# Input products of a triangular inverse as 64x64 matmuls in place of 64x32 quarters

## The chip, the cores and the metric

The kernel runs on one core of one Trainium2 chip. The metric is the device time of one launch in microseconds (us): the median of three runs is 1617.11 us (1615.75 to 1618.56). TensorE (PE) multiplies matrices into PSUM, VectorE (DVE), ScalarE (ACT) and GpSimd (POOL) do the elementwise work, SyncE (SP) issues DMAs. Each engine takes its instructions strictly in the order in which they stand in its queue, and waits on semaphores for the others.

## The reference, cut to what matters

Two transformer-like blocks follow each other on 512 tokens of width 1024. The first has a mixer with a convolution branch and a recurrence (RWKV, 8 heads of width 64, both directions, over 256 context tokens and then 512 tokens); the second has another recurrence, windowed attention and a feed-forward part. The change touches the recurrence of the first:

```python
def wkv_scan(state0, r, decay, kk, b, v, k, reverse):
    def step(S, inp):
        r_t, w_t, kk_t, b_t, v_t, k_t = inp
        sa = jnp.einsum("bhvk,bhk->bhv", S, kk_t)
        S = (S * w_t[:, :, None, :] - sa[..., None] * b_t[:, :, None, :]
             + v_t[..., None] * k_t[:, :, None, :])
        return S, jnp.einsum("bhvk,bhk->bhv", S, r_t)
```

The kernel does 64 tokens at a time (a chunk; 12 chunks, the first 4 of context). Inside a chunk the steps depend on each other through a 64x64 strictly triangular matrix A = (keys kk) x (b), and the chunk needs the inverse of (1 + A). The result is the same function; only how A is computed and stored changes.

## The kernel before, in words

Heads are taken two at a time: `j` = 0 to 3, one head in partitions 0 to 63, the other in 64 to 127. For each `j` there are two pieces of work.

`prep(j)` makes the inputs: decays and keys for both directions `d` (activations on ACT, a scan and some products on DVE, into `KB` and `KR`), then the products for the inverse (line 633, PSUM tile `pa`), and then calls `inverse(j)`. A is stored in quarters of 32x32: the two blocks on the diagonal go to `AKD`, the two off it to `AKO`, for 24 matrices (12 chunks, 2 directions). Every quarter is a matmul of its own: 64 rows of contraction, 32 output rows, 32 columns. Twelve chunks by two quarters by two heads are 48 matmuls, then ACT copies the PSUM tile out (line 638), once for `AKD` and once for `AKO`. `AKO` has two buffers, `AKD` one.

`inverse(j)` inverts the diagonal 32x32 blocks by 31 steps of substitution on DVE (lines 670 and 671, two instructions a step, 124 of each for the four `j`), between a transpose into `U` (line 662) and two out of `X` (`F1`, `F2`, lines 673 and 674), and then forms the off-diagonal block with two rounds of 32x32 matmuls (`pt`, lines 691, from `AKO` and `F2`, copied by ACT to `T`; and `po`, lines 698 and 699), copied into `XT`.

`stage(j)` runs the recurrence with the finished inputs: 12 groups, each one chunk of both directions, as a chain matmul, ACT copy `RU` (line 756), matmul with `XT`, ACT copy `RU` (762), matmul, ACT copy into the state `S` (768). All its matmuls go through `mmh` (line 644): two 64x64 matmuls, one a head. For every second group `pair` makes scores (`psc`, masked by a DVE copy into `AS`, line 731) and transposes (`pkt`, copied by ACT to `kbt`).

`prep(0)` and the start of `prep(1)` run beside the projections of `proj`, which are 128x128 matmuls. The rest of `prep(1)`, and `prep(2)`, run beside stage 0, `prep(3)` beside stage 1. Both generators are cut by `yield`s into steps; `stage` takes `RB` = 4, 2, 1, 1 steps after each group of stages 0 to 3, with priorities, and a scheduler then orders each engine's queue. When the inverse of `prep(3)` is done, its memory becomes the pools of the next phase: `ada12` streams 32 weight tiles of 512 KB (line 539) and reduces each with one DVE instruction (line 540) beside stages 2 and 3, and the loads of the output projection `wout` (line 156) stand behind them in SP's queue.

Of the kernel before, what the change touches and what calls it, by code (L numbers as in the profile page):

```python
# [10 lines left out]
F32 = mybir.dt.float32  # L11
# [7 lines left out]
P = 128  # L19
# [103 lines left out]
class K:  # L123
# [120 lines left out]
    def build(self):  # L244
        tc = self.tc
        with ExitStack() as es:
            self.dr = es.enter_context(tc.tile_pool(name="dr", bufs=1, space=bass.MemoryType.DRAM))
            self.ea = es.enter_context(ExitStack())
            p0 = self.p0 = self.pool(es, "p0", side="left")
            self.cst = p0.tile([P, NCST], F32, name="cst")  # L250
            self.vec = p0.tile([P, NVEC], F32, name="vec")
            self.mod = p0.tile([P, 48, 2], F32, name="mod")
            self.scz = p0.tile([P, KD, 32], F32, name="scz")
            self.mhalf = p0.tile([P, 16], F32, name="mhalf")
            zxb = p0.tile([P, KD, NX], F32, name="zx")
            self.zx = [zxb[:, k, :] for k in range(KD)]
            with ExitStack() as er:
                r0 = self.r0 = self.pool(er, "r0", side="left")
                self.sg = r0.tile([P, NX], F32, name="sg")
                self.vD = self.dr.tile([P, 4, 12, 64], F32, name="vD")  # L260
                self.rD, self.kD, self.kkD = [[self.dr.tile([P, n], F32, name=f"{t}D{j}") for j in range(4)] for t, n in (("r", NX), ("k", NT), ("kk", NT))]
                st = lambda p, name, shape: p.tile([P] + shape, F32, name=name)
                XT0, XT1 = self.XT0, _ = st(r0, "XT0", [24, 64]), zxb[:, 5:8, :].rearrange("p a (b c) -> p (a b) c", c=64)
                set0 = {"KB": [st(r0, f"KB0{d}", [12, 2, 64]) for d in range(2)], "KR": [st(r0, f"KR0{d}", [1280]) for d in range(2)]}
                self.sets = [dict(set0, XT=XT0), {"XT": XT1}, None, dict(set0, XT=XT0)]
                self.hb, self.kah = st(r0, "hb", [16]), st(r0, "kah", [4, 4])
                with ExitStack() as ep:
                    self.pp = self.pool(ep, "pp", side="right")
                    self.lin = [self.pp.tile([P, NT], F32R, name=f"lin{i}") for i in range(2)]

                    room = [(f"KB1{d}", 6) for d in range(2)] + [("KR10", 5)]
                    self.room = []
                    for tag, n in room:
                        t = self.pp.tile([P, n, NC_], F32, tag=tag, name="adaw", bufs=1).rearrange("p a b -> p (a b)")
                        self.room += [t[:, i * 512:i * 512 + 512].unsqueeze(1) for i in range(n // 2)]
                    self.psp = self.psum(ep, "psp", side="right")
                    self.AKD = st(self.pp, "AKD", [32, 32])
                    with ExitStack() as e1:
                        self.wp = self.r1 = self.pool(e1, "r1", side="left")
                        self.ps = self.psum(e1, "ps1")  # L280
                        self.mmbufs, self.axbufs, self.wbufs, self.wsbufs = 4, 2, 4, 3
                        self.proj()
                    r2 = self.r2 = self.pool(er, "r2", side="left")
                    self.ps2 = self.psum(er, "ps2")
                    self.sets[2] = {"KB": [st(r2, f"KB2{d}", [12, 2, 64]) for d in range(2)], "KR": [st(r2, f"KR2{d}", [1280]) for d in range(2)], "XT": st(r2, "XT2", [24, 64])}
                    self.rwkv(es, ep)
            self.tail()
# [11 lines left out]
    def proj(self):  # L299
        nc, A, r1, p0 = self.nc, self.A, self.r1, self.p0  # L300
# [47 lines left out]
        for kc in range(KD):  # L348
# [4 lines left out]
            for i in range(2):  # L353
# [5 lines left out]
                    nc.gpsimd.tensor_tensor(out=hlo[i][kc], in0=xT[i][kc], in1=hhi[i][kc].bitcast(F32), op=ALU.subtract)  # L359
                else:  # L360
                    nc.vector.scalar_tensor_tensor(out=hlo[i][kc], in0=xT[i][kc], scalar=sh, in1=hhi[i][kc].bitcast(F32), op0=ALU.add, op1=ALU.subtract)
        nc.gpsimd.memset(self.AKD, 0.0)

        def tile_of(u, x=True, c=True):
            ws = [ahead.pop((u, k0), None) or piece(u, k0) for k0 in (0, 4)]
# [15 lines left out]
        for i, t in enumerate(self.lin):  # L381
            r = slice(64 * i, 64 * i + 64)
# [60 lines left out]
        for tb in range(6):  # L443
            t = r1.tile([P, NX], F32, tag="vs", name="v", bufs=4)
            nc.scalar.activation(out=t, in_=pv[tb], func=AF.Copy)
            for i in range(4):
                r, hs = slice(64 * (i % 2), 64 * (i % 2) + 64), slice(64 * (i // 2), 64 * (i // 2) + 64)
# [6 lines left out]
        for j in range(4):  # L454
            t = self.zx[j]
# [89 lines left out]
    def prep(self, j):  # L545
        nc, pp = self.nc, self.pp
# [22 lines left out]
        nc.scalar.activation(out=bo, in_=pb, func=AF.Copy)  # L569
        S["bo"] = bo  # L570
        ch = lambda t: t.rearrange("p (c t) -> p c t", t=64)
        AKO = S["AKO"] = pp.tile([P, 24, 32], F32, tag="AKO", name="AKO", bufs=2)
        for d in range(2):
            def lora(i, out, bias):

# [46 lines left out]
            nc.vector.tensor_tensor(out=krx[:, :, 1, :], in0=ch(rt), in1=inc[:, 4:12, :], op=ALU.mult)  # L622
            yield

            for off, A in enumerate((self.AKD, AKO)):
                pa = psm(384, "pa")
                for c in range(12):
                    kp = krc[:, c, :] if c < 4 else krx[:, c - 4, 0, :]
                    lt, rt_ = (kp, kb[:, c, bs, :]) if d else (kb[:, c, bs, :], kp)
                    for q in range(2):  # L630
                        o, i = 32 * q, 32 * (q ^ off)
                        for h in (0, 64):
                            nc.tensor.matmul(pa[h + o:h + o + 32, c * 32:c * 32 + 32], lt[h:h + 64, o:o + 32], rt_[h:h + 64, i:i + 32], start=True, stop=True)
                    if c == 5:
                        yield
                self.copy(nc.scalar, A[:, 12 * d:12 * d + 12, :], pa.rearrange("p (c t) -> p c t", t=32))
                yield
        yield from self.inverse(j)

# [14 lines left out]
    def inverse(self, j):  # L654

        nc, pp = self.nc, self.pp
        big = lambda name: pp.tile([P, 32, 32], F32, tag="inv", name=name, bufs=3)
        XT, AKO = self.S[j]["XT"], self.S[j]["AKO"]  # L660
        U, tmp, X = big("U"), big("tmp").rearrange("p a b -> p (a b)"), big("X")
        nc.vector.transpose(out=U, in_=self.AKD.rearrange("p n i -> p i n"))
        nc.gpsimd.memset(X, 0.0)
        nc.gpsimd.memset(X.rearrange("p a b -> p (a b)")[:, ::33], 1.0)
        for k in range(31):
            if k % 4 == 0:
                yield
            n, w = 31 - k, k + 1
            tv = tmp[:, 0:n * w].rearrange("p (a b) -> p a b", b=w)
            nc.vector.tensor_tensor(out=tv, in0=U[:, k + 1:32, k:k + 1].to_broadcast([P, n, w]), in1=X[:, k:k + 1, 0:w].to_broadcast([P, n, w]), op=ALU.mult)  # L670
            nc.vector.tensor_tensor(out=X[:, k + 1:32, 0:w], in0=X[:, k + 1:32, 0:w], in1=tv, op=ALU.subtract)
        F1, F2 = big("F1"), big("F2")
        nc.vector.transpose(out=F1.rearrange("p n i -> p i n"), in_=X)
        nc.vector.transpose(out=F2.rearrange("p n j -> p j n"), in_=X.rearrange("p i j -> p j i"))
        yield
        b0, b1 = [slice(o, o + 32) for o in (0, 64)], [slice(o + 32, o + 64) for o in (0, 64)]
        D = slice(0, 12), slice(12, 24)
        for r, F in zip(D, (F1, F2)):
            self.copy(nc.vector, XT[:, r, :].rearrange("p n (q i) -> p n q i", q=2), F[:, r, :].unsqueeze(2).to_broadcast([P, 12, 2, 32]))
        for h in range(2):  # L680
            nc.gpsimd.memset(XT[b1[h], D[0], 0:32], 0.0)
            nc.gpsimd.memset(XT[b0[h], D[1], 32:64], 0.0)

        T = big("T")
        ps = lambda name: self.psp.tile([P, 12, 32], F32, tag="inv", name=name, bufs=1)
        for r in D:
            yield
            pt = ps("pt")
            for n in range(r.start, r.stop):
                for h in range(2):  # L690
                    nc.tensor.matmul(pt[b1[h], n - r.start, :], AKO[b0[h], n, :], F2[b0[h], n, :], start=True, stop=True)
            for h in range(2):
                self.copy(nc.scalar, T[b1[h], r, :], pt[b1[h]])
        yield
        po = ps("po")
        for c in range(12):
            for h in range(2):
                nc.tensor.matmul(po[b0[h], c, :], T[b1[h], c, :], F1[b1[h], c, :], start=True, stop=True)
                nc.tensor.matmul(po[b1[h], c, :], F1[b1[h], 12 + c, :], T[b1[h], 12 + c, :], start=True, stop=True)
        for h in range(2):  # L700
            self.copy(nc.scalar, XT[b0[h], D[0], 32:64], po[b0[h]], -1.0)
            self.copy(nc.scalar, XT[b1[h], D[1], 0:32], po[b1[h]], -1.0)
# [692 lines left out]
```

## Time and profile before

| what | value |
|---|---|
| median of three runs | 1617.11 us |
| profiled execution: its time, its span | 1620.11 us, 1618.3 us |
| mean granted PE clock over the span | 0.969 |
| busy: PE, DVE, ACT, POOL | 1533.4, 998.3, 629.8, 116.8 us |
| `proj` with `prep(0)`, until the first group of stage 0 | 0 to 261 us |
| stage 0, stage 1, stage 2, stage 3 | 261 to 338, 338 to 430, 430 to 492, 492 to 551 us |

The span runs from the first instruction to the last; 1.8 us of the execution's time lie outside it. A granted clock of 1.00 is TensorE's level of 2.4 GHz, 0.50 is 1.2 GHz. A PE that the profile calls busy has a matmul in flight; that doesn't say that the array is full. A row of the timeline merges neighbours of one form: start, duration, engine, line, operation, out<-in, array rows*columns of a matmul, shape, count, and in brackets the idle time before it with what ended it.

### The profile page before, as it was taken

The numbers are of one execution on the slowest core, as the hardware profiler recorded it, in microseconds if no ns is written. First come the engines' busy times: TensorE is split into PE (matmuls) and PEld (weight loads), VectorE is DVE, ScalarE is ACT, GpSimd is POOL, SyncE is SP. The second block draws the span as 40 slices with busy tenths as digits, with TensorE's granted clock in tenths as the row PEclk, the third lists the DMA queues.
The fourth block names the chain that finished last, engine by engine and source line by source line (L and its number), as shares of the span: only waits on it lengthen the run. The fifth ranks groups of instructions, "written<-read, shape, count | busy, mean of one in ns | idle before, by whom it ended". The sixth has DMA issues, their size and how long they took to land. (4 is left out here: it accounts for less than half of the span.)

```text
span 1618.3 us, 31205 instructions
## 1 busy us (share of the span) xinstructions
PE 1533.4 (95%) x13214; PEld 1254.0 (77%) x13214; DVE 998.3 (62%) x1689; ACT 629.8 (39%) x1258; POOL 116.8 (7%) x133
## 2 busy tenths in 40 slices
PE   4999999899988899999999997999999999999998
PEld 2877777788777699888888885887677888888886
DVE  3447758873577478888883437678965555554221
ACT  3524344454244344333332335334554333333222
POOL 1111000110101000000000004121200000000000
PEclk9999999797689999999999999999999999999999
DMA  9243321100138442323223332211022222323321
GB/s 333 85 155 101 105 85 57 35 13 4 38 108 258 152 142 80 104 91 104 92 89 94 95 101 69 90 56 51 27 66 91 92 91 91 103 93 92 104 82 61
DMA packets 62188, 152.98 MB, mean 95 GB/s; under 512 B 12640, under 2 KB 14432, under 8 KB 62048
## 3 DMA queue, kind: packets, MB, share of 16 engines
q1 hardware_dynamic: 58016, 143.95, 27.6%
q10 hardware_dynamic: 4032, 7.04, 1.3%
q8 instruction: 103, 1.69, 0.4%
q14 instruction: 37, 0.30, 0.1%
HBM read 143.10 MB, written 7.86 MB: 93 GB/s over the span
## 5 line engine op out<-in xcount | busy, mean ns | idle before, releaser
L181 ACT ACTIVATE whi<-w 128x1024 fp32r<-128x1024 f32 (+2 forms) x220 | 209.0, 952 | 453.6 <-PE pm L170 336.2
L182 DVE TENSOR_TENSOR wlo<-w,whi 128x1024 fp32r<-128x1024 f32 (+2 forms) x212 | 229.5, 1084 | 211.5 <-ACT whi L181 206.8
L169 PE MATMUL pm<-ahi,whi 128*128 128x512 f32 (+1 forms) x624 | 236.5, 379 | 2.6 <-DVE sh L1078 2.2
L170 PE MATMUL pm<-alo,whi 128*128 128x512 f32 (+1 forms) x624 | 234.8, 376 | 0.0
L171 PE MATMUL pm<-ahi,wlo 128*128 128x512 f32 (+1 forms) x624 | 234.0, 375 | 0.0
L170 PE MATMUL pm<-al,whi 128*128 128x512 f32 x352 | 139.7, 397 | 0.0
L169 PE MATMUL pm<-ah,whi 128*128 128x512 f32 x352 | 139.2, 395 | 0.0
L171 PE MATMUL pm<-ah,wlo 128*128 128x512 f32 x352 | 139.2, 395 | 0.0
L169 PEld LDWEIGHTS pm<-ahi,whi 128*128 128x128 f32 x624 | 117.6, 188 | 23.9 <-ACT sh L1093 2.6
L171 PEld LDWEIGHTS pm<-ahi,wlo 128*128 128x128 f32 x624 | 117.6, 188 | 20.9 <-issue 0.7
L170 PEld LDWEIGHTS pm<-alo,whi 128*128 128x128 f32 x624 | 117.6, 189 | 20.0 <-issue 0.7
L951 DVE SCALAR_TENSOR_TENSOR cv<-pm,vec,cv 128x441 f32<-128x441 f32 (+2 forms) x176 | 121.1, 693 | 4.1
L171 PEld LDWEIGHTS pm<-ah,wlo 128*128 128x128 f32 x352 | 66.2, 188 | 16.1 <-issue 0.2
L170 PEld LDWEIGHTS pm<-al,whi 128*128 128x128 f32 x352 | 66.2, 188 | 16.1 <-issue 0.2
L169 PEld LDWEIGHTS pm<-ah,whi 128*128 128x128 f32 x352 | 66.2, 188 | 16.0
L169 PE MATMUL pm<-hhi,whi 128*128 128x512 f32 x176 | 71.3, 405 | 0.5 <-ACT whi L181 0.5
L171 PE MATMUL pm<-hhi,wlo 128*128 128x512 f32 x176 | 70.6, 401 | 1.0 <-DVE wlo L182 1.0
L170 PE MATMUL pm<-hlo,whi 128*128 128x512 f32 x176 | 69.9, 397 | 0.0
L169 PE MATMUL pd<-whi,gh 128*128 128x512 f32 x176 | 69.5, 395 | 0.0
L169 PE MATMUL pm<-hh,whi 128*128 128x512 f32 x176 | 69.3, 394 | 0.0
L170 PE MATMUL pm<-hl,whi 128*128 128x512 f32 x176 | 69.3, 394 | 0.0
L171 PE MATMUL pm<-hh,wlo 128*128 128x512 f32 x176 | 69.3, 394 | 0.0
(397 smaller groups left out, 3140.2 us busy)
## 6 DMA issues: line engine op xcount, KB each, us to landing
w<-in_fup SPq DMA_DIRECT2D x44, 512.0 KB, 3.4
adaw<-in_adat SPq DMA_DIRECT2D x32, 512.0 KB, 4.6
w<-in_win SPq DMA_DIRECT2D x44, 256.0 KB, 2.9
w<-in_wg SPq DMA_DIRECT2D x22, 512.0 KB, 3.4
w<-in_wu SPq DMA_DIRECT2D x22, 512.0 KB, 3.4
w<-in_wd SPq DMA_DIRECT2D x22, 512.0 KB, 3.6
w<-in_win SPq DMA_DIRECT2D x18, 512.0 KB, 3.4
w<-in_wout SPq DMA_DIRECT2D x16, 512.0 KB, 3.8
```

The source lines that it names most:

```text
L169: nc.tensor.matmul(out, lh, rh, start=(first and i == 0), stop=False)
L170: nc.tensor.matmul(out, lh, rl, start=False, stop=False)
L171: nc.tensor.matmul(out, ll, rh, start=False, stop=(last and i == n - 1))
L181: self.nc.scalar.activation(out=hi, in_=src, func=AF.Copy)
L182: (eng or self.nc.vector).tensor_tensor(out=lo, in0=src, in1=hi.bitcast(F32), op=ALU.subtract)
L951: nc.vector.scalar_tensor_tensor(out=o, in0=p[:, ro[0] + dr:ro[1] + dr, co[0] + dc:co[1] + dc], scalar=w(i), in1=o, op0=ALU.mult, op1=ALU.add)
```

## The change

The quarters go. For each direction, `prep` makes two PSUM tiles of six chunks each, with the same `mmh` as everywhere in the stages: one 64x64 matmul a head and chunk. ACT copies the whole 64x64 blocks into one tile `AK` [128, 32, 64] that all `j` share (one buffer). At the start of `inverse`, GpSimd moves, for the lower 32 rows of either head, the diagonal block from columns 32 to 63 to columns 0 to 31, so that `AK[:, :, 0:32]` is what `AKD` was; the upper rows' columns 32 to 63 are what `AKO` was for the matmuls of `pt`. There are two `yield`s a direction in place of four, and one more in `inverse`: 29 steps for a `prep` in place of 32.

```diff
-                    self.AKD = st(self.pp, "AKD", [32, 32])
+                    self.AK = st(self.pp, "AK", [32, 64])
...
-        AKO = S["AKO"] = pp.tile([P, 24, 32], F32, tag="AKO", name="AKO", bufs=2)
...
-            for off, A in enumerate((self.AKD, AKO)):
+            for q in range(2):
                 pa = psm(384, "pa")
-                for c in range(12):
+                for c in range(6 * q, 6 * q + 6):
                     kp = krc[:, c, :] if c < 4 else krx[:, c - 4, 0, :]
                     lt, rt_ = (kp, kb[:, c, bs, :]) if d else (kb[:, c, bs, :], kp)
-                    for q in range(2):
-                        o, i = 32 * q, 32 * (q ^ off)
-                        for h in (0, 64):
-                            nc.tensor.matmul(pa[h + o:h + o + 32, c * 32:c * 32 + 32], lt[h:h + 64, o:o + 32], rt_[h:h + 64, i:i + 32], start=True, stop=True)
-                    if c == 5:
-                        yield
-                self.copy(nc.scalar, A[:, 12 * d:12 * d + 12, :], pa.rearrange("p (c t) -> p c t", t=32))
+                    self.mmh(pa[:, (c - 6 * q) * 64:(c - 6 * q) * 64 + 64], lt, rt_)
+                n = 12 * d + 6 * q
+                self.copy(nc.scalar, self.AK[:, n:n + 6, :], pa.rearrange("p (c t) -> p c t", t=64))
                 yield
...
+        for h in range(2):
+            nc.gpsimd.tensor_copy(out=AK[b1[h], 0:24, 0:32], in_=AK[b1[h], 0:24, 32:64])
+        yield
...
-        nc.vector.transpose(out=U, in_=self.AKD.rearrange("p n i -> p i n"))
+        nc.vector.transpose(out=U, in_=AK[:, :, 0:32].rearrange("p n i -> p i n"))
...
-                    nc.tensor.matmul(pt[b1[h], n - r.start, :], AKO[b0[h], n, :], F2[b0[h], n, :], start=True, stop=True)
+                    nc.tensor.matmul(pt[b1[h], n - r.start, :], AK[b0[h], n, 32:64], F2[b0[h], n, :], start=True, stop=True)
```

The order of the queues, before and after. First PE's queue in stage 1, where the second direction of `prep(3)` forms its products (`pa`) beside the pairs of stage 1 (`psc`, `pkt`). A row is line, operation, out<-in, output shape and count. Before:

```order
L644 MATMUL pkt<-cst,KB_1789 64x64
L633 MATMUL pa<-KB_85,KR_87 32x32 x2
L644 MATMUL psc<-KR_1792,KB_1790 64x128
L633 MATMUL pa<-KB_85,KR_87 32x32
L644 MATMUL psc<-KR_1792,KB_1790 64x128
L633 MATMUL pa<-KB_85,KR_87 32x32
```

The same products after, with the matmuls of the recurrence (`c`) around them:

```order
L639 MATMUL c_2378<-vt,kbt 64x64
L639 MATMUL pa<-KB_85,KR_87 64x64 x4
L639 MATMUL c_2375<-vt,AS_2366 64x64 x2
L639 MATMUL c_2375<-S_2373,KR_1648 64x64 x2
L639 MATMUL c_2377<-RU_2369,kbt 64x64 x2
L639 MATMUL c_2375<-RU_2369,AS_2366 64x64 x2
L639 MATMUL c_2376<-vt,AS_2368 64x64
L639 MATMUL pa<-KB_85,KR_87 64x64 x12
```

Where single 32x32 quarters alternated with 64x64 matmuls, there are now runs of 4 and 12 of the one form, all 64x64. Over the whole program a change of array form stands between neighbours in PE's queue 267 times before and 100 times after.

Second, ACT's queue in stage 0, where the inverse of `prep(1)` ends (`T`, and `zx`, which holds that `XT`) and `prep(2)` copies its products out. Before:

```order
L188 ACTIVATE T<-pt 32x384 x4
L188 ACTIVATE zx<-po 32x12x32 x4
L188 ACTIVATE AKD<-pa 128x384
L188 ACTIVATE kbt<-pkt 128x256
L756 ACTIVATE RU_2633<-c_2639 128x64
```

After:

```order
L755 ACTIVATE RU_2370<-c_2375 128x64
L188 ACTIVATE AK<-pa 128x384
L188 ACTIVATE T<-pt 32x384 x2
L761 ACTIVATE RU_2370<-c_2375 128x64
L188 ACTIVATE T<-pt 32x384 x2
L188 ACTIVATE AK<-pa 128x384
L767 ACTIVATE S_2373<-c_2377,pc 128x64
```

Before, the copies for the second direction follow the end of the inverse (those of the first stand 28 rows earlier). After, these are the copies of the first direction: each stands where the `pt` matmuls of the inverse before it have read the part of `AK` that it overwrites.

Third, DVE's queue where the inverse of `prep(3)` begins with `U`; the copies into `AS` are those of the pairs. Before, `U` stands among the pairs of stage 1 (the copies into 384 columns belong to late groups):

```order
L616 TENSOR_TENSOR KB_85<-b_4709,sg 128x12x64
L731 COPY_PREDICATED AS_2629<-cst,psc 128x384
L731 COPY_PREDICATED AS_2631<-cst,psc 128x384
L662 STREAM_TRANSPOSE U<-AKD 128x1024
L670 TENSOR_TENSOR tmp<-U,X 128x31
```

After, the copies around it belong to the first pair of stage 2 (its context chunks have 2x64 columns):

```order
L615 TENSOR_TENSOR KB_85<-b_4163,sg 128x12x64
L621 TENSOR_TENSOR KR_87<-rt,cs 128x8x64
L730 COPY_PREDICATED AS_2367<-cst,psc 128x2x64
L662 STREAM_TRANSPOSE U<-AK 128x1024
L670 TENSOR_TENSOR tmp<-U,X 128x31
```

`U` has moved from ahead of the last pair of stage 1 to behind the first pair of stage 2.

## Rows read from the trace of the kernel before

**Rows 1.** Windows by stage: length, busy us (instructions) of PE, PEld, DVE, ACT, POOL; clock; DMA.

```profile
261.00:338.00 77.00, 69.23 (x1770) 59.63 (x1772) 60.22 (x136) 36.85 (x130) 6.12 (x12) 0.87 0.06 20
338.00:430.00 92.00, 89.98 (x1726) 72.17 (x1724) 46.09 (x95) 37.09 (x126) 7.14 (x13) 0.78 0.03 8
430.00:492.00 62.00, 55.18 (x1332) 48.28 (x1330) 45.69 (x93) 30.33 (x115) 5.93 (x7) 0.89 0.38 124
492.00:551.00 59.00, 49.19 (x1122) 41.95 (x1116) 40.11 (x68) 25.82 (x104) 4.90 (x3) 1.00 0.76 240
```

**Rows 2.** Waits in stage 1 (338 to 430 us): total us, times, longest.

```profile
DVE AS L731 <- PE psc L644: 28.4, 6, 11.2
ACT kbt L188 <- PE pkt L644: 12.0, 7, 8.4
DVE U L662 <- ACT AKD L188: 8.1, 1, 8.1
```

**Rows 3.** PE's timeline at full clock, stage 1.

```profile
400.08 0.28 PE L644 MATMUL c<-S,KR 64*64 64x64 f32 x4
400.20 0.28 PE L644 MATMUL c<-RU,kbt 64*64 64x64 f32 x4
...
400.64 0.24 PE L633 MATMUL pa<-KB,KR 64*32 64x32 f32 x2
400.82 0.32 PE L644 MATMUL c<-vt,AS 64*64 64x64 f32 x2
401.07 0.24 PE L633 MATMUL pa<-KB,KR 64*32 64x32 f32 x2
```

**Rows 4.** PE's timeline at half clock, stage 1.

```profile
409.06 0.31 PE L633 MATMUL pa<-KB,KR 64*32 64x32 f32 x2
...
409.70 0.31 PE L633 MATMUL pa<-KB,KR 64*32 64x32 f32 x2
...
421.44 0.31 PE L633 MATMUL pa<-KB,KR 64*32 64x32 f32 x2
...
422.38 0.42 PE L644 MATMUL c<-vt,AS 64*64 64x64 f32 x4
422.59 0.42 PE L644 MATMUL c<-S,KR 64*64 64x64 f32 x4
```

**Rows 5.** The first switch into the quarters' form in the stages, PE's timeline.

```profile
285.86 0.57 PE L633 MATMUL pa<-KR,KB 64*32 64x32 f32 x42
```

**Rows 6.** The products `pa` by window: busy us (instructions) of PE, PEld, ACT; clock; DMA.

```profile
120.00:261.00 141.00, 8.77 (x768) 7.55 (x768) 3.78 (x8) 1.00 0.33 100
338.00:430.00 92.00, 18.15 (x384) 11.11 (x384) 1.97 (x4) 0.78 0.03 8
```

**Rows 7.** One block of quarters at full clock beside the projections, PE's timeline.

```profile
138.28 1.02 PE L633 MATMUL pa<-KR,KB 64*32 64x32 f32 x96
```

**Rows 8.** GpSimd by line and form: count, busy us, mean ns, idle before.

```profile
L564 POOL TENSOR_TENSOR rk<-rt,kt 128x512 f32<-128x512 f32 x4 | 5.4, 1357 | 20.9 <-PE pnb L411 12.1 <-DMA rt<-rD 4.9 <-DVE X L671 4.0
L1127 POOL COPY kz<-ak 64x512 f32<-64x512 f32 x4 | 3.5, 878 | 13.7 <-ACT ak L1119 13.6
```

**Rows 9.** DVE's timeline beside GpSimd's work of 337.2 to 339.7 us.

```profile
336.46 0.42 DVE L671 TENSOR_TENSOR X<-X,tmp 128x256 f32<-128x256 f32 x1
...
337.68 0.85 DVE L671 TENSOR_TENSOR X<-X,tmp 128x255 f32<-128x255 f32 x1
```

**Rows 10.** DVE's timeline: `U` and the end of the inverse of `prep(3)`.

```profile
403.60 1.93 DVE L662 STREAM_TRANSPOSE U<-AKD 128x1024 f32<-128x1024 f32 x1 [8.13 <-ACT AKD L188]
...
453.67 1.98 DVE L674 STREAM_TRANSPOSE F<-X 128x1024 f32<-128x1024 f32 x1
```

**Rows 11.** Line 540, the reductions of `ada12`: ns min/median/max, first and last start.

```profile
L540 DVE SCALAR_TENSOR_TENSOR adaw<-adaw,cb x32: 1208/1224/1939, 471.3 to 533.8; 128x1024 f32<-128x1024 f32 x32
```

**Rows 12.** Line 156 from 525 us: weights of `wout`, issues and landing.

```profile
L156 SPq DMA_DIRECT2D w<-in_wout x4: 327/327/328, 531.8 to 538.4; - x4
...
DMA to landing us min/median/max: 4.2/4.7/6.5
```

More of the change, by code (lines that the diff above doesn't have):

```diff
@@ L361, in proj @@
                     nc.vector.scalar_tensor_tensor(out=hlo[i][kc], in0=xT[i][kc], scalar=sh, in1=hhi[i][kc].bitcast(F32), op0=ALU.add, op1=ALU.subtract)
-        nc.gpsimd.memset(self.AKD, 0.0)
+        nc.gpsimd.memset(self.AK, 0.0)
         def tile_of(u, x=True, c=True):
@@ L659, in inverse @@
         big = lambda name: pp.tile([P, 32, 32], F32, tag="inv", name=name, bufs=3)
-        XT, AKO = self.S[j]["XT"], self.S[j]["AKO"]
+        XT, AK = self.S[j]["XT"], self.AK
+        b0, b1 = [slice(o, o + 32) for o in (0, 64)], [slice(o + 32, o + 64) for o in (0, 64)]
+        for h in range(2):
+            nc.gpsimd.tensor_copy(out=AK[b1[h], 0:24, 0:32], in_=AK[b1[h], 0:24, 32:64])
+        yield
         U, tmp, X = big("U"), big("tmp").rearrange("p a b -> p (a b)"), big("X")
-        nc.vector.transpose(out=U, in_=self.AKD.rearrange("p n i -> p i n"))
+        nc.vector.transpose(out=U, in_=AK[:, :, 0:32].rearrange("p n i -> p i n"))
         nc.gpsimd.memset(X, 0.0)
@@ L675, in inverse @@
         yield
-        b0, b1 = [slice(o, o + 32) for o in (0, 64)], [slice(o + 32, o + 64) for o in (0, 64)]
         D = slice(0, 12), slice(12, 24)
```

## The prediction

> **What bounds the kernel now.** I read the windows by stage first. Outside the recurrence of the first block nothing changes but buffer numbers, so the question is the stretch from 120 to 551 us. The four stages do the same recurrence, and yet last 77, 92, 62 and 59 us [rows 1]. Stage 3 has no `prep` beside it and 1,122 matmul records; stage 1 has 1,726 records and 384 of them are `pa` [rows 1, 6]. So 1,342 other records take it 92 us, where stage 3 does 1,122 in 59. In stage 1 DVE is busy 46 of 92 us and ACT 37, while PE has a matmul in flight 90 of 92 and its mean granted clock is 0.78 [rows 1]. The view of waits says the same from the other side: DVE's copies into `AS` waited 28.4 us for `psc` in six waits, ACT's copies to `kbt` 12.0 us for `pkt`, DVE's `U` 8.1 us for the copy of `pa` [rows 2]. All three wait for PE. Stage 1 is bound by PE, with little multiplying in it.
>
> PE's timeline shows why. Four 64x64 records follow the four before them after 0.12 us at full clock (400.08 to 400.20) and 0.21 us at half (422.38 to 422.59). Where two records of a 64x32 quarter stand between two pairs of 64x64 records, one round takes 0.43 us at full clock (400.64 to 401.07) and 0.64 at half (409.06 to 409.70) [rows 3, 4]. Each change of the array's form empties the array first. A round trip thus costs 0.43 - 0.12 = 0.31 us at full clock, 0.64 - 0.21 = 0.43 at half. From the first at 285.86 to the last at 421.44 [rows 5, 4] I counted 70 switches into the quarters' form from 64x64 and 72 back, so 71 round trips: in stage 0 five at full and 9.5 at half clock, in stage 1 26.5 and 30.
>
> **The change part by part.**
>
> *Round trips gone.* `pa` gets the form of its neighbours, and the queue shows it in runs of 4, 8 and 12. 31.5 x 0.31 + 39.5 x 0.43 = 9.8 + 17.0 = 26.8 us, of which stage 0 has 5.6 and stage 1 has 21.2. Is it on the path? In stage 1 yes: waits of 28.4 us stand on `psc`, the very matmuls between which the quarters lie. In stage 0 DVE is busy 60 of 77 us, and a part may be covered. I take 27, bounds 15 (half of stage 0's and two thirds of stage 1's) and 27.
>
> *The clock.* Mean 0.78 over 92 us is 40 us at the lower level (2 x 0.22 x 92), 0.87 over 77 is 20. The half-clock round trips themselves fill 39.5 x 0.64 = 25 of these 60; the other 35 us would be up to 17 shorter at full clock. The clock fell in stretches where PE stood in switches or waited, so some comes back; but waits for the inverse's end also remain. Bounds 0 and 17, I take 6.
>
> *The products themselves.* Beside the projections (120 to 261 us) eight blocks of quarters take 8.77 us [rows 6]. A block is 48 matmuls, 96 records, 1.02 us [rows 7], about 10.6 ns a record: four quarters run at once. A block of the new form is 12 matmuls, 24 records at 0.12 / 4 = 0.03 us, with the last one's 0.2 us tail 0.9. So 8 x (1.1 - 0.9) = 1.6 us, I take 1.5. The column time is nearly the same, as four 32-column quarters side by side become two 64-column halves. The Trainium skill (TensorEngine Tiling (Array Packing), Instruction Overhead) has about 60 cycles for each matmul, so that short ones cost as much as long ones. By that rule a quarter would cost what a 64x64 matmul does, the eight blocks would fall to a quarter of 8.77 us, 6.6 less, and the sum would be -25.6 in place of -20.5 us. The rows speak against it where tiles run side by side: 10.6 ns a record against 30.
>
> *GpSimd's copies.* Two for each `prep`, 32 partitions x 768 elements, between ACT's last copy and `U`. No row has this form. The nearest is a copy of 512 elements at 878 ns; scaled by 768/512 it is 1.3 us. Bounds: 0.9, that row as it is, and 2.0, the product of 512 elements with two inputs (1357 ns) scaled likewise [rows 8]. So 1.8 to 4 us a `prep`, I take 2.6. `prep(0)` is covered by projections. In the other three DVE has `U` next in its queue, and behind it stand the steps of substitution and the next pair's copies into `AS`, for which PE waits. Two per `prep` only delay it: 3 x 2 = 6 us with what the added `yield` lets DVE do before; bounds 0 (the other work of DVE fills it) and 12. Beside GpSimd, DVE itself slows: the substitution step of 0.42 us took 0.85 [rows 9]. The Trainium skill (SBUF — State Buffer, SBUF: two separate sides) calls the port that GpSimd shares with DVE an exclusive lock, held for a whole instruction against DVE instructions with two SBUF inputs. By that rule eight copies could hold DVE up to 8 x 1.3 = 10 us beyond my 6; here `U` is what DVE stands at while they run, so I add nothing; with the 10 the sum would be -10.5.
>
> *One buffer for A.* The copies of `prep(j+1)`'s first direction now wait for the `pt` matmuls of `inverse(j)`, and as all products of `prep` share one PSUM buffer, its second direction starts only after that. Hence `U` of `prep(3)` moves from 403.6 us in stage 1 [rows 10] to behind the first pair of stage 2. The end of this inverse (`F2` ends at 455.65, 26 us into stage 2) frees the memory for `ada12`, whose first reduction comes 16 us later; 32 of them run from 471.3 to 533.8, one each 2.0 us at the pace of their loads, and the output projection's weights are issued behind, from 531.8 to 538.4, landing 4.7 us later [rows 10 to 12]. That is some 8 us before the recurrence ends at 551. From 403.6 to 430, DVE did `U` and the first steps, some 10 us, which now lie in stage 2, and the second direction's products for `KB` and `KR` with them, some 8 more. So `F2` ends some 18 us later into stage 2, and behind it the reductions and the weights; of that the 8 us of room cover a part, and stage 3 gives some back, because DVE is busy 40 of its 59 us [rows 1]. Bounds 0 and 18, I take 8.
>
> *Sum.* -27 - 6 - 1.5 + 6 + 8 = -20.5 us. The profiled execution (1620.1) would come to 1599.6; the median of the runs, 3.0 below it, from 1617.1 to 1596.6.
>
> **The rivals.**
>
> *All of it and the clock too.* Without switches PE leaves the path, the clock stays up, and stage 1 falls to the pace of stage 3, 59 us, stage 0 to 66 (DVE's 60 and its waits): -33 - 11 - 1.5 + 8 = -37.5, or 1579.6. For it: DVE and ACT are busy half of stage 1 or less. Against it: the ends of the inverses still chain DVE, PE, ACT (`F2`, `pt`, `T`, `po`) in every stage. 0.20.
>
> *The switches were cover.* The recurrence then waits for `prep`'s chain instead: `pa`, copies, GpSimd, `U`, 62 instructions of substitution. DVE's queued work stays, and its waits move from `psc` to `U`. Half of the trips' 27 us come back as time, and GpSimd and the single buffer take 6 + 8: 1617.1 - 13.5 - 1.5 + 14 = 1616. 0.14.
>
> *Slower: the single buffer.* If the substitution of `inverse(3)` goes beside the pairs of stage 2 at the pace it has now (403.6 to 455.65, 52 us), `F2` ends 52 us into the stage in place of 26. The stream of 62 us and the weights are then the end of the block, whatever stage 3 does, and they come 26 us later, less the 8 of room: 18 against what stages 0 and 1 save together. Below 18 us of savings the kernel is slower. With 10 saved, 1617.1 + 18 - 10 - 1.5 = 1623.6. Against it: the trips alone give 27, and the pairs that slowed the substitution were themselves late. 0.11.
>
> That the change doesn't do what it says can be left out: the queue has `pa` as 64x64 throughout, and 100 changes of form in place of 267.
>
> **How the numbers follow.** My forecast has 0.55, the rivals 0.20, 0.14 and 0.11. The time is that of the forecast, 1596.6. Its own range is 1586 to 1608: the clock's term at 17 below, and above it the single buffer at 18. The 8-in-10 range reaches to the large gain below, with a little room for a clock that comes back whole, and above to just short of the cover case: 1574 to 1613. About 0.2% (3.2 us) is what a measurement of this kernel can tell from no change. Faster: 0.55 + 0.20 and 0.05 of the cover case = 0.80. Within 0.2%: 0.07, nearly all of it the cover case. Slower: 0.13, the last rival and a rest of the cover case.
>
> **What would show it.** Right: no form 64x32 left on PE; stage 1 at 60 to 75 us with DVE's wait for `psc` below 10 us; mean clock of stage 1 above 0.85; the first reduction of `ada12` before 465 us. GpSimd's copies near 1.3 us, and DVE's wait before `U` naming GpSimd, 2 to 5 us a time. The rival of the large gain: clock 1.0 through stages 0 and 1, and stage 1 at 60. The cover case: stage 1 near 85, with its waits on `U`. The last: stage 1 shorter, but the first reduction after 471 us. Wrong altogether would be stretches outside 120 to 551 that differ by more than 3 us, or a round from `pa` to its neighbours that costs PE as much as before though the forms agree.

## The result, and the profile after

The changed kernel takes 1589.23 us (median of 4 runs, 1586.77 to 1598.46) where the kernel before took 1616.43 (median of 4): the ratio is 0.9832, with a 95% interval of 0.9807 to 0.9857. The gain is 27 us; the forecast was 20.5, its range 1574 to 1613.

The profiled execution of the changed kernel took 1588.74 us with a span of 1586.9, so 31.4 less than the span before. Where they went is read from the first `RU` of each stage (now line 755). The stages begin at 261.4, 324.0, 397.7 and 462.8 us; before at 261.9, 338.2, 430.8 and 493.2. With the last `RU` at 515.5 (before 549.7) this gives:

| stretch | before | after | difference |
|---|---|---|---|
| up to stage 0 | 261.9 | 261.4 | -0.5 |
| stage 0 | 76.3 | 62.6 | -13.7 |
| stage 1 | 92.6 | 73.7 | -18.9 |
| stages 2 and 3, to the last `RU` | 118.9 | 117.8 | -1.1 |
| the rest | 1068.6 | 1071.4 | +2.8 |

The windows of the four stages after, with the columns of [rows 1]:

```profile
261.40:324.00 62.60, 58.76 (x1385) 50.58 (x1386) 46.55 (x99) 35.51 (x124) 5.75 (x13) 0.92 0.07 23
324.00:397.70 73.70, 67.48 (x1474) 57.12 (x1470) 52.61 (x107) 38.15 (x128) 11.74 (x15) 0.86 0.04 10
397.70:462.80 65.10, 58.06 (x1356) 52.26 (x1354) 47.97 (x106) 31.10 (x117) 6.91 (x8) 0.84 0.23 77
462.80:517.00 54.20, 46.18 (x1088) 39.44 (x1086) 41.36 (x75) 21.99 (x100) 3.99 (x4) 1.00 0.80 253
```

Stage 1 has fewer matmul records (1,474, where [rows 1] has 1,726), and its clock went from 0.78 to 0.86. The two stages divide the gain unlike the forecast (5.6 and 21.2 us of round trips) because a piece of work crossed the border: `U` of `prep(2)`, with the substitution behind it, began 23 us before the end of stage 0 and now begins 1.3 us before it.

```profile
315.45 1.95 DVE L662 STREAM_TRANSPOSE U<-AKD 128x1024 f32<-128x1024 f32 x1 [4.32 <-ACT AKD L188]
```

The row above is DVE's timeline of before, the one below that of after:

```profile
322.70 1.95 DVE L662 STREAM_TRANSPOSE U<-AK 128x1024 f32<-128x1024 f32 x1 [1.84 <-POOL AK L659]
```

Waits in stage 1 after (324 to 397.7 us), against [rows 2]:

```profile
DVE AS L730 <- PE psc L639: 12.3, 4, 8.2
ACT kbt L188 <- PE pkt L639: 8.7, 6, 2.6
```

DVE waits 12.3 us for `psc` where it waited 28.4, and `U` of `prep(3)` no longer waits 8.1 us for a copy behind slow quarters. But one wait of 8.2 us is left; the run with two buffers, below, bears on it. The products beside the projections, with the columns of [rows 6], and one block of them on PE's timeline, against [rows 7]:

```profile
120.00:261.40 141.40, 7.59 (x192) 6.40 (x192) 3.94 (x8) 0.98 0.32 97
```

```profile
135.88 0.92 PE L639 MATMUL pa<-KR,KB 64*64 64x64 f32 x24
```

They take 7.59 us in place of 8.77. GpSimd's copies (duration ns min/median/max, first and last start) and who waited for them (us, times), then the reductions of `ada12`, against [rows 11]:

```profile
L659 POOL COPY AK<-AK x8: 815/822/829, 148.5 to 395.5; 32x768 f32<-32x768 f32 x8
...
  DVE U L662: 5.8, 4
```

```profile
L540 DVE SCALAR_TENSOR_TENSOR adaw<-adaw,cb x32: 1201/1224/1679, 451.4 to 515.8; 128x1024 f32<-128x1024 f32 x32
```

### The profile page after: what moved, and what is told of

Same layout as the page of the kernel before. It is cut to its first block, busy times and chain, and to the rows that moved or that the text cites. A ratio compares the mean times of both kernels' runs of the same rounds, so it can differ in the third digit from the quotient of the medians.

```text
span 1586.9 us, 28915 instructions
## 1 busy us (share of the span) xinstructions
PE 1503.9 (95%) x12062; PEld 1235.6 (78%) x12062; DVE 1000.5 (63%) x1689; ACT 631.3 (40%) x1258; POOL 124.0 (8%) x141
## 5 line engine op out<-in xcount | busy, mean ns | idle before, releaser
L169 PEld LDWEIGHTS pm<-ahi,whi 128*128 128x128 f32 x624 | 117.9, 189 | 24.5 <-ACT sh L1092 3.0
```

What stands on the lines that cost most here:

```text
L169: nc.tensor.matmul(out, lh, rh, start=(first and i == 0), stop=False)
```

## The experiments

Theory F is that of the prediction: a change of array form between neighbours in PE's queue costs 0.31 to 0.43 us a round trip, and those are gone. Two rivals would give the same result. Rival O: the products left the gaps of the recurrence, and their form is of no account. Rival C: there are fewer matmuls (24 for a direction in place of 96). Edits are to the changed kernel, where nothing else is said.

**Quarters again, all else as changed.**

```diff
-                    self.mmh(pa[:, (c - 6 * q) * 64:(c - 6 * q) * 64 + 64], lt, rt_)
+                    e = (c - 6 * q) * 64
+                    for o in (0, 32):
+                        for i in (0, 32):
+                            for h in (0, 64):
+                                nc.tensor.matmul(pa[h + o:h + o + 32, e + i:e + i + 32], lt[h:h + 64, o:o + 32], rt_[h:h + 64, i:i + 32], start=True, stop=True)
```

> The changed kernel with every 64x64 product made of four 64x32 quarters again (192 matmuls a prep as before, and all else as changed: one buffer, GpSimd's copies, fewer steps). Its PE queue has the quarters in 19 runs in place of 81 before. Theory F (each change of array form between neighbours costs 0.31 to 0.43 us a round trip): few changes are left, so it stays near the changed kernel, 1590 to 1596 us, ratio to before 0.984 to 0.988. Rival O (what counts is that the products left the gaps of the recurrence, whatever their form): the same. Rival C (what counts is the number of matmuls, 48 a direction fewer issues): 1612 to 1617, ratio 0.997 to 1.0.

Measured 1593.80 us, ratio 0.9832 (0.9805 to 0.9858): the changed kernel's own. (The matmuls fewer for a direction are 72, not the 48 of the expectation.) C falls for quarters, and so does the simple reading of F, that the new form brought the gain. Without any new form the gain is there. The trace has 9 switches from 64x64 into the quarters in the stages in place of 70, because with one buffer the queue has the products in whole blocks. A block of 96 records takes little longer than 24 of 64x64 do:

```profile
136.09 1.11 PE L633 MATMUL pa<-KR,KB 64*32 64x32 f32 x96
```

**Both forms, in the same blocks.** One head of each chunk as a 64x64 matmul, the other as four quarters.

```diff
-                    self.mmh(pa[:, (c - 6 * q) * 64:(c - 6 * q) * 64 + 64], lt, rt_)
+                    e = (c - 6 * q) * 64
+                    nc.tensor.matmul(pa[0:64, e:e + 64], lt[0:64], rt_[0:64], start=True, stop=True)
+                    for o in (64, 96):
+                        for i in (0, 32):
+                            nc.tensor.matmul(pa[o:o + 32, e + i:e + i + 32], lt[64:128, o - 64:o - 32], rt_[64:128, i:i + 32], start=True, stop=True)
```

> The changed kernel with the two heads of each chunk in different forms: one 64x64 matmul, then four 64x32 quarters, 12 changes of form per six chunks, 96 round trips in all, half of them beside the projections and half in the stages. The products stand in 22 runs in PE's queue, as in the changed kernel (21) and in the one with quarters alone (19). Theory F (a change of form between neighbours costs time, 0.31 to 0.43 us a round trip): 96 x 0.31 to 0.43 = 30 to 41 us more than the changed kernel, 1619 to 1631 us, ratio to before 1.000 to 1.008. Rival O (only the place of the products in the queue counts, either form alone having given the same time): 1589 to 1597, ratio 0.983 to 0.987.

Measured 1636.96 us, ratio 1.0114 (1.0083 to 1.0144). Each form alone gives 0.983, in about as many blocks (19 and 21, here 22); the two mixed give 1.011. That decides between F and O: the change of form is what costs. It isn't the count either: this kernel has 60 matmuls for a direction, the one with quarters alone 96. 1.0114 - 0.9832 is 2.8% of the 1619.5 us of before, 46 us for 96 round trips, 0.48 us each, where F had expected 30 to 41 us in all. This has the clock in it. Stage 0 starts at 290.3 us here, 28.9 later than in the changed kernel; the products before it, half of all, are these (columns of [rows 6]):

```profile
120.00:290.30 170.30, 28.24 (x480) 21.52 (x480) 3.93 (x8) 0.88 0.27 82
```

They keep PE busy 20.7 us longer than the 7.59 above, 0.43 for each of the 48 round trips. The other 8 us go with a mean clock of 0.88 in place of 0.98, which the projections' own matmuls have too. PE's timeline of this kernel, at full and at half clock:

```profile
134.65 0.32 PE L630 MATMUL pa<-KR,KB 64*64 64x64 f32 x2
134.91 0.32 PE L633 MATMUL pa<-KR,KB 64*32 64x32 f32 x8
135.16 0.33 PE L630 MATMUL pa<-KR,KB 64*64 64x64 f32 x2
...
139.27 0.47 PE L630 MATMUL pa<-KR,KB 64*64 64x64 f32 x2
139.67 0.43 PE L633 MATMUL pa<-KR,KB 64*32 64x32 f32 x8
140.03 0.47 PE L630 MATMUL pa<-KR,KB 64*64 64x64 f32 x2
```

Two and eight records take 0.51 us at full clock, 0.76 at half. By the blocks above they would take 2 x 0.04 + 8 x 0.012 = 0.17 without the switches. The Trainium skill (TensorEngine Tiling (Array Packing), Key Properties) says that changing the tiling mode drains the engine. The trace agrees, and puts 0.51 - 0.17 = 0.34 us on the round trip at full clock.

**As many matmuls as before, all 64x64.** First in the changed kernel, each product cut into four of 16 columns.

```diff
-                    self.mmh(pa[:, (c - 6 * q) * 64:(c - 6 * q) * 64 + 64], lt, rt_)
+                    e = (c - 6 * q) * 64
+                    for i in range(0, 64, 16):
+                        self.mmh(pa[:, e + i:e + i + 16], lt, rt_[:, i:i + 16])
```

> The changed kernel with each 64x64 product cut into four matmuls of 64 rows by 16 columns: as many matmuls as before (96 a direction), in the 64x64 form, in 21 runs. Theory F and rival O: as the changed kernel, 1588 to 1594 us, ratio 0.982 to 0.987. Rival C: back to 1612 to 1617, ratio 0.997 to 1.0.

Measured 1637.21 us, ratio 1.0099 (1.0066 to 1.0133). All three theories would have it otherwise than measured: F and O expected no change, C only a return to 1617. A 64x16 record costs what a 64x64 record does:

```profile
135.19 3.08 PE L641 MATMUL pa<-KR,KB 64*64 64x16 f32 x96
```

96 records in 3.08 us are 32 ns each; the 24 in 0.92 above are 38, with the last one's tail. So C holds where the form is 64x64. `pa` keeps PE busy for 65.7 us in place of 17.1, and the 48.6 between them are about the whole loss (the medians differ by 48.0). The Trainium skill (TensorEngine Tiling (Array Packing), Instruction Overhead) has an overhead of about 60 cycles a matmul, so that one column takes as long as 60. These rows agree in that 16 columns take as long as 64; the quarters (96 in 1.11 us, 11.6 ns each, four side by side) are quicker than that rule. Whether it is the matmul or its weight load that sets the 32 ns isn't told apart here: beside PE's 65.7 us the weight loads take 63.8.

Then in the kernel before, at its own interleaved places:

```diff
-                        o, i = 32 * q, 32 * (q ^ off)
+                        i = 32 * off + 16 * q
                         for h in (0, 64):
-                            nc.tensor.matmul(pa[h + o:h + o + 32, c * 32:c * 32 + 32], lt[h:h + 64, o:o + 32], rt_[h:h + 64, i:i + 32], start=True, stop=True)
+                            nc.tensor.matmul(pa[h:h + 64, c * 32 + 16 * q:c * 32 + 16 * q + 16], lt[h:h + 64, 0:1].to_broadcast([64, 64]), rt_[h:h + 64, i:i + 16], start=True, stop=True)
```

> The kernel before, with the products in the 64x64 form alone: as many matmuls, at nearly the same places in PE's queue (89 runs, most of them single matmuls between those of the recurrence), 64 output rows by 16 columns in place of 32 by 32; buffers, copies and DVE's queue as before. The 64 weight columns of each are one column repeated, so A is not the reference's. Theory F: the round trips vanish, 1588 to 1599 us, ratio 0.982 to 0.990, and stage 1 takes 65 to 75 us. Rivals O and C: nothing changes, 1612 to 1620 us, stage 1 stays at 92.

Measured 1634.20 us, ratio 1.0072 (1.0043 to 1.0102): F's total was missed, for the reason just found. Stage 0 starts at 291.2 us, 29 late, about as in the run above (292.4), since the same narrow matmuls stand beside the projections, and takes 83.0 us in place of 76.3. Stage 1 is another matter:

```profile
374.20:449.90 75.70, 72.09 (x1742) 63.63 (x1739) 46.01 (x96) 37.09 (x128) 7.89 (x14) 0.89 0.04 9
```

1,742 records, as many as before (1,740 from 338.2 to 430.8 us), nearly the same queue, each product dearer; and yet 75.7 us in place of 92.6, at a clock of 0.89 in place of 0.78. Stage 1 behaves as F says; the whole kernel doesn't, so this run alone would prove nothing.

**Two buffers for A.**

```diff
-                    self.AK = st(self.pp, "AK", [32, 64])
+                    self.AKs = [st(self.pp, f"AK{i}", [32, 64]) for i in range(2)]
...
-        XT, AK = self.S[j]["XT"], self.AK
+        XT, AK = self.S[j]["XT"], self.AKs[j % 2]
```

> The changed kernel with two tiles AK in place of one, taken in turn by j. If the single buffer costs what the prediction put on it (8 us), 1581 us or less, ratio 0.978, with U of prep(3) earlier than 394 us. If the buffer costs nothing: 1586 to 1592, ratio 0.982 to 0.985. If the second direction's products, free to start earlier, only go back between the matmuls of the recurrence (26 runs in the queue) and cost time there: 1592 or more.

Of these the first came true: 1579.82 us, and `U` of `prep(3)` starts at 371.6 us, where it was 396.4 in the changed kernel.

> Two tiles AK taken in turn, and every 64x64 product made of four 64x32 quarters: against the run with two buffers (1579.8 us, ratio 0.9747) only the form differs, against the run with quarters and one buffer (0.9832, as the changed kernel) only the buffer. With the second buffer the queue has the quarters in 83 runs, some 60 of them of one or two between the matmuls of the recurrence. Theory F: some 65 round trips at 0.31 to 0.49 us, 20 to 32 us more than with 64x64, 1600 to 1612 us, ratio 0.987 to 0.994: the second buffer then turns from a gain into a loss. If only the buffer counts and the form doesn't: 1578 to 1584.

Measured 1612.68 us, ratio 0.9943: what F expects, a little over the upper end of its range (1612). The changed kernel ran once more beside the second of these:

> The changed kernel once more, on the same chip as the run beside it, as the base of the comparisons: 1586 to 1592 us, ratio 0.981 to 0.986 by every theory.

It took 1591.77 us, ratio 0.9808 (0.9785 to 0.9832), and its stages 0 and 1 62.7 and 76.3 us. The four together, as medians and ratios to the kernel before:

| | one buffer | two buffers |
|---|---|---|
| 64x32 quarters | 1593.80; 0.9832 (0.9805 to 0.9858) | 1612.68; 0.9943 (0.9925 to 0.9960) |
| 64x64 | 1589.23; 0.9832 (0.9807 to 0.9857) | 1579.82; 0.9747 (0.9725 to 0.9770) |

Along the bottom row the second buffer saves about 10 us by the medians (14 by the ratios), along the top row it costs 19 (18). Down the left column the form does nothing that is clear of the intervals, down the right it is worth 1.96% of 1620, 32 us. With the second buffer the products are free early, and the queue puts them one by one between the matmuls of the recurrence. With quarters each such place costs a round trip (350 to 353 us, PE):

```profile
351.46 0.24 PE L634 MATMUL pa<-KR,KB 64*32 64x32 f32 x2
351.63 0.32 PE L644 MATMUL psc<-KR,KB 64*64 64x64 f32 x2
351.89 0.24 PE L634 MATMUL pa<-KR,KB 64*32 64x32 f32 x2
```

0.43 us a round, that of [rows 3], of which 0.31 is the price of the trip. The trace has 75 such switches in the stages, and 32 / 75 = 0.43 us for each; this has the clock's loss in it, as stage 1 has 0.84 here and 1.00 with 64x64. With 64x64 the same interleaving costs next to nothing:

```profile
366.36 0.22 PE L640 MATMUL pa<-KB,KR 64*64 64x64 f32 x1
366.41 0.22 PE L640 MATMUL pkt<-cst,KB 64*64 64x64 f32 x1
366.41 0.27 PE L640 MATMUL pa<-KB,KR 64*64 64x64 f32 x2
366.47 0.22 PE L640 MATMUL pkt<-cst,KB 64*64 64x64 f32 x1
```

Stages 0 and 1 by windows, first with quarters, then with 64x64, two buffers both:

```profile
264.70:333.00 68.30, 61.46 (x1711) 53.26 (x1707) 54.77 (x124) 37.19 (x127) 18.77 (x14) 0.93 0.07 23
333.00:426.20 93.20, 90.45 (x1740) 71.96 (x1738) 51.32 (x106) 37.32 (x128) 10.49 (x16) 0.84 0.03 8
```

```profile
264.00:325.00 61.00, 57.09 (x1414) 49.86 (x1416) 52.95 (x117) 35.58 (x124) 7.47 (x14) 0.94 0.08 25
325.00:388.90 63.90, 58.35 (x1462) 49.56 (x1456) 54.94 (x120) 37.16 (x128) 17.70 (x16) 1.00 0.04 10
```

What the single buffer costs in the changed kernel stands in its timeline, in that wait of 8.2 us:

```profile
370.40 0.49 ACT L188 ACTIVATE AK<-pa 128x384 f32<-128x384 f32 x1 [2.10 <-PE pt L690]
370.52 0.57 DVE L730 COPY_PREDICATED AS<-cst,psc 128x384 f32<-128x384 int32 x1
...
371.06 0.75 PE L639 MATMUL pa<-KR,KB 64*64 64x64 f32 x18
...
371.95 1.36 PE L690 MATMUL pt<-F,AK 32*32 32x32 f32 x48
...
374.35 0.49 ACT L188 ACTIVATE AK<-pa 128x384 f32<-128x384 f32 x1
...
377.12 1.96 ACT L188 ACTIVATE XT<-po 32x384 f32<-32x384 f32 x4 [2.06 <-PE po L698]
...
379.30 0.59 DVE L730 COPY_PREDICATED AS<-cst,psc 128x384 f32<-128x384 int32 x1 [8.20 <-PE psc L639]
...
383.18 0.62 DVE L190 TENSOR_SCALAR sg<-sg,cst 128x768 f32<-128x768 f32 x1 [3.29 <-ACT sg L579]
```

The copies into `AK` wait for `pt` (370.40), the second block of `pa` and the second direction's first matmuls wait for these, all in PE's queue ahead of the next `psc`, while DVE has no substitution left and stands still for 11.5 of 12 us (371.1 to 383.2). The end of the inverse (`T`, `po`, `XT`) stands in the same stretch, and the timeline doesn't divide the 8.2 us between it and the buffer; that the buffer is what costs is shown by the other run. With two buffers none of the seven longest waits of stage 1 is for `psc`.

**GpSimd's share.** ACT puts the diagonal blocks in place itself, in four copies for one, with one buffer and with two; and with two buffers, ACT makes GpSimd's two copies.

```diff
-                self.copy(nc.scalar, self.AK[:, n:n + 6, :], pa.rearrange("p (c t) -> p c t", t=64))
+                pv = pa.rearrange("p (c t) -> p c t", t=64)
+                for h in (0, 64):
+                    self.copy(nc.scalar, self.AK[h:h + 32, n:n + 6, :], pv[h:h + 32])
+                    self.copy(nc.scalar, self.AK[h + 32:h + 64, n:n + 6, 0:32], pv[h + 32:h + 64, :, 32:64])
...
-        for h in range(2):
-            nc.gpsimd.tensor_copy(out=AK[b1[h], 0:24, 0:32], in_=AK[b1[h], 0:24, 32:64])
```

```diff
-            nc.gpsimd.tensor_copy(out=AK[b1[h], 0:24, 0:32], in_=AK[b1[h], 0:24, 32:64])
+            self.copy(nc.scalar, AK[b1[h], 0:24, 0:32], AK[b1[h], 0:24, 32:64])
```

> The changed kernel without GpSimd's copies: ACT evicts each PSUM tile in four copies in place of one, the lower rows' diagonal blocks straight to columns 0 to 31. DVE's U waited 5.8 us in all for GpSimd, of it some 4 in the stages; ACT gets about 4 x 1.2 = 4.6 us a prep. If GpSimd's copies cost what the prediction put on them (6 us): 1583 us, ratio 0.980. If the wait was covered and ACT is off the path too: 1587 to 1591, ratio 0.982 to 0.984. If ACT's copies delay the recurrence's: 1592 to 1600.

> Two tiles AK taken in turn, and ACT's four copies in place of GpSimd's move. With two buffers alone the time was 1579.8 (ratio 0.9747). If GpSimd's move is still 4 us on the path: 1575, ratio 0.972. If it is covered: 1578 to 1582. If ACT's longer work takes it back: 1583 or more.

> Two tiles AK taken in turn, the move of the diagonal blocks by two ACT copies of 32x768 in place of two on GpSimd (0.82 us each there). ACT is through in about 1.5 us but has its own queue, with the recurrence's copies in it. If GpSimd's share of DVE's port or its latency matters: 1575 to 1578, ratio 0.972 to 0.974. If not: 1578 to 1584.

Measured 1592.59 us, ratio 0.9843 (0.9818 to 0.9867); 1597.99, 0.9866 (0.9845 to 0.9888); and 1580.03, 0.9763 (0.9740 to 0.9787). None is faster than its base (0.9832, and 0.9747 for the two others). Each puts work on ACT in GpSimd's place, so they show that GpSimd's move costs no more than these do, not that it is free; the four copies on ACT are 18 us slower with two buffers. Why so much isn't settled: ACT is busy 81 us in stages 0 and 1 in place of 73, the stages take 70 and 75 us in place of 61 and 64, and `U` of `prep(3)` starts at 392.4 us in place of 371.6, nearly as late as with one buffer.

## Why the prediction was right, and where not

*Round trips and clock, -27 and -6.* Stages 0 and 1 together are 32.6 us shorter, against 33 forecast, the mean clock of stage 1 is 0.86 (over 0.85 was named), and no 64x32 form is left. One sign was missed: DVE's wait for `psc` in stage 1 is 12.3 us, and below 10 was named. And the agreement is two errors that cancel. With the second buffer the two stages take 61.0 and 63.9 us, 44 less than before, and the single buffer took 11 of this back in the same stages, where the prediction had no price for it. Of the 44 the form is worth 36.6: with quarters and two buffers the stages take 68.3 and 93.2 us, and only the form differs. So much the trips and the clock were worth, where 27 + 6 = 33 were taken. The other 7 us the kernel with quarters has too, though it has as many switches as before (75 and 70); no run says where they come from. The price of a trip held (0.43 us between the kernels with two buffers, 0.48 in the mixed one, both with the clock's loss in them; 0.31 and 0.43 were read from the timeline). How the 36.6 divide between trips and clock no run shows: if the trips took their 27, the clock gave 10, between the 6 taken and its bound of 17. And what takes the trips away is told only half. The prediction gave it to the new form; the single buffer would have done it without the form, and together they gain no more than the buffer alone.

*The products, -1.5.* 8.77 - 7.59 = 1.2 us, and stage 0 starts 0.5 earlier. Between them lies a stretch at half clock, 187.9 to 194.7 us, which the kernel before doesn't have.

*GpSimd's copies, +6.* A copy takes 0.82 us, below the 1.3 taken and the lower bound of 0.9: 24 times 32 elements in 32 partitions are quicker than 512 in 64. `U` waited 5.8 us in four times (2 to 5 each were named): 2.3 and 0.7 beside the projections, 1.8 and 0.9 in the stages, so at most 2.7 of the 6 lay there. None of the three kernels without the move is faster, though ACT does it in GpSimd's place. The bound of nothing is nearest.

*One buffer, +8.* This step failed in its place and mechanism. The prediction had the price at the end of stage 3, through the later stream of `ada12`. That stream did start later in its stage, 53.7 us after the start of stage 2 in place of 40.5, and yet stages 2 and 3 together are 1.1 us shorter. Nor does an earlier stream shorten them: with two buffers it starts 36.1 us after the start of stage 2 (388.9), and the two stages take 117.9 us, with one buffer 117.8.

```profile
L541 DVE SCALAR_TENSOR_TENSOR adaw<-adaw,cb x32: 1204/1224/2095, 425.0 to 488.7; 128x1024 f32<-128x1024 f32 x32
```

The price stands in stage 1, 73.7 us in place of 63.9, where the inverse's end and the next products wait for each other; its size, 9.4 us by the medians (1589.23 - 1579.82), was near, by luck.

*The sum.* In the profiled executions -31.4 us where -20.5 was forecast. The 10.9 between them, term by term: +1.0 before stage 0 (0.5 won in place of 1.5), +0.4 in stages 0 and 1, -6 for GpSimd, -9.1 in stages 2 and 3 (1.1 won in place of 8 lost), and +2.8 after the recurrence, which the prediction had unchanged. Some of that last may be the clock: it stands at half from 966.1 to 969.5 us, a stretch more than before. The medians differ by less, 27.2 us, because the profiled execution of before was 3.7 above its median and that of after 0.5 below.

*The rivals.* The large gain (1579.6, the clock at 1.00 and stage 1 near 60) is what two buffers with the new form give: 1579.82, and in stage 1 1.00 and 63.9. The cover case had stage 1 near 85 with waits on `U`: neither is there. The slower one wanted the first reduction after 471 us: it came at 451.4.

## What to carry to other kernels

When PE is called busy and its stage still runs far below what its matmuls are worth, look at the form of neighbours in its queue: single matmuls of another form between the main ones cost a third to a half of a microsecond a round trip here, whatever they compute. Then there are two cures, one form for all or whole blocks of the odd form, and a buffer more is a gain or a loss by which of them is in place. So change form and buffers in a two by two table before giving a gain to one of them; and don't cut matmuls of 64 rows into narrower ones.

The version to keep is the new form with two buffers and GpSimd's move: 1579.82 us, 0.9747 of the kernel before.

## What was not expected of the hardware

- A 64x64 matmul record of 16 columns takes 32 ns, as long as one of 64 columns (38 with the tail); a 64x32 quarter takes 11.6 ns.
- After the long blocks of 16-column matmuls beside the projections the granted clock fell to half in stretches that are at full clock before (138 to 148, 158 to 169, 203 to 213 and 240 to 250 us). Stage 0 started 31 us later than in the changed kernel; 23 of them are the blocks themselves (30.8 us of PE in place of 7.6). After the blocks of the mixed kernel, which have no narrow matmuls, it fell too (138 to 148, 158 to 165, 199 to 209 and 240 to 247 us).
- GpSimd's copy of 768 elements in 32 partitions took 0.82 us, the one of 512 elements in 64 partitions 0.88 [rows 8].
